# A hybrid decoder trunk: when the last down weights are split, where six bias products stand, and how the modulation products are spread

## The chip, the cores and the metric

The kernel runs on one core of a Trainium2 chip. The metric is the device time of one launch in microseconds, from the inputs in DRAM to the output in DRAM, as a median of several runs. The engines are TensorE (PE), VectorE (DVE), ScalarE (ACT), GpSimd (POOL) and SyncE (SP), which issues most of the transfers.

## What is computed

One layer on x with 512 positions and 2048 features, all in f32. A vector c gives six modulation vectors of 2048 values each; the rest is two residual blocks and a final norm.

```python
mod = silu(c) @ ada_w + ada_b          # shift1, scale1, gate1, shift2, scale2, gate2
h = rms_norm(x, g1) * (1 + scale1) + shift1
q, f, i, g, u = split(h @ w_in)        # 4 x 1024 and 1024 columns
y_a = hgrn2(q, f, i, g)                # 8 heads, chunkwise recurrence
y_b = multi_scale_pool(u)              # trailing means, windows 2, 4, 8, 16
x = x + gate1 * (concat(y_a, y_b) @ w_out)
h = rms_norm(x, g2) * (1 + scale2) + shift2
a, v = split(h @ w_up)                 # 2 x 5632 columns
x = x + gate2 * ((silu(causal_conv3(a)) * v) @ w_down)
out = rms_norm(x, g_final)
```

## The kernel before

All data lie with features on the 128 partitions and the 512 positions along the free axis. Every f32 product is made of three products of rounded halves (`mm3`, L138): each operand is split into a high part, cast on ACT, and a low part, subtracted on DVE. Weights of 128 x 1024 are split by `split_weights` (L107, lines 110 and 111 in the profile), activations and the last weights by `split` (L164, lines 166 and 167). A tile of 128 outputs is summed over k in one PSUM bank and then evicted by DVE or ACT.

The program is written as one straight order. A scheduler places each instruction on its engine by that order and by when its operands and buffers are expected to be free; on the chip each engine then runs its own queue in order. The buffers that matter: nine raw buffers of 128 x 1024 f32, 512 KB each (`rp`, L43), which hold every loaded weight, the rows of the vector products, broadcast vectors and the output blocks; three pairs of split weights (`wp`, L44); 73 tiles of 128 x 512 (`tp`, L42).

The stages, in the order of time:

- The modulations are vector products: `ada_tile` (L99) loads 1 MB of `ada_w` as two raw buffers through `gemv` (L90), and DVE multiplies each by the broadcast silu(c) and sums along the free axis (L95). `adaq` (L555) lists them. `mk_side` (L557) returns a function that the matrix loops call after every four k steps; with `adas=0.25` every fourth call makes one modulation product (`ada_next`, L568).
- The input projection, in several parts. Its last part makes the gate g in eight tiles of 16 k steps (L634 to L640), with the recurrence of the heads pumped between.
- The output projection in two passes of 16 tiles with 8 k steps each. Pass 1 (L646 to L667) takes the pooled half, adds gate1 times the sum to x and reads x again from DRAM; pass 2 (L681 to L689) takes the recurrent half, and also makes the sum of squares and the scaled, split input `h2` of the next block.
- The up projection begins with NP0 = 3 plain tile pairs (`up_mm`, L694, 96 x 3 matmuls of 512 columns over the three k parts of each pair). They work on x scaled but not shifted, so that each of their six output rows needs a bias afterwards: the product of the weights with shift2. `bias2` (L867) makes it, again through `gemv`; the first call also broadcasts shift2 over the partitions (`bcast_vec`, L521: a transpose on PE, a copy, a store to DRAM and two loads into raw buffers). Beside plain pair 1 the generator `make_a` (L822) makes the normed input, beside pair 2 `make_h` (L835) makes the seven operands of the next stage in seven steps.
- The other 41 pairs run in groups of seven half products (`up_group`, L898, in the order `SEQ` = P1, Q5, P2, P7, Q3, P6, Q4, each 24 matmuls of 256 columns). `Fast` (L727) loads, adds and splits their weights at written steps ahead; one addition per operand is made by an accumulating load from GpSimd (L766). After P2 and Q3 of the groups 1 to 5 one item of the list `todo` (L894) runs: two calls of `bias2` and then `late` (L878), the convolution and gate of a plain pair, for each of the three pairs.
- The down projection in five chunks of 10, 10, 10, 10 and 4 k blocks (`JD`, L22). In the first four, `Down.get` (L950) loads a unit of eight blocks six units ahead and splits it three ahead. The last chunk works on the two halves of the positions in turn, with 16 features of 12 matmuls of 256 columns each. In its first half every second feature loads and splits one unit of weights (L1026 to L1030); the second half uses them again. Then come the final norm and the stores.

Lines of this text and of the profile are those of the kernel before.

Of the kernel before, what the change touches and what calls it, by code (L numbers as in the profile page):

```python
# [8 lines left out]
F32 = mybir.dt.float32  # L9
# [3 lines left out]
ALU = mybir.AluOpType  # L13

P = 128
T = 512
# [19 lines left out]
def trunk_kernel(ctx: ExitStack, tc: tile.TileContext, x, c, ada, w_in, w_qft, pool_w, w_out, w_up, w_dn, cst, msk, out):  # L36
# [52 lines left out]

    def gemv(src, vec):  # L90
        a = sp.tile([P, 2], F32, tag="acc", bufs=4, name="acc")
        for i in range(2):
            r = rp.tile([P, U], F32, tag="raw", name="raw")
            nc.sync.dma_start(r, src[:, i * U:(i + 1) * U])
            V.scalar_tensor_tensor(out=r, in0=r, scalar=1.0, in1=vec[i], op0=ALU.mult, op1=ALU.mult,  # L95
                                   accum_out=a[:, i:i + 1])
        return a
# [535 lines left out]
    gs = []  # L633
    sd = mk_side(pumps=1, adas=0.25, pools=1)  # L634
    for hd in range(8):
# [9 lines left out]
    hs = [split(ys.pop(k)) for k in range(NH, 2 * NH)]  # L645
    sd = mk_side(pumps=1, adas=0.25)  # L646

# [32 lines left out]

    sd = mk_side(adas=0.5)  # L681
    ssa = tt()
# [182 lines left out]
    vec2 = []  # L865

    def bias2(i):  # L867
        if i == 0:
            vec2.append(bcast_vec(mods[3]))
        a = gemv(w_qft[KT + i], vec2[0])  # L870
        V.tensor_tensor(biases[:, KT + i:KT + i + 1], a[:, 0:1], a[:, 1:2], op=ALU.add)
        V.tensor_scalar(raws[i], raws[i], biases[:, KT + i:KT + i + 1], None, ALU.add)
        if i == 2 * NP0 - 1:
            vec2.clear()

    ad = dp.tile([NJ, P, T], F32, tag="ad", name="ad", bufs=1)

    def late(jj):  # L878
        nc.sync.dma_start(ad[jj], glu(jj, raws[2 * jj], raws[2 * jj + 1]))
        raws[2 * jj] = raws[2 * jj + 1] = None  # L880

    for jj in range(NP0):
        pr = up_mm(h2, mid if jj == 0 else None, (lambda: next(ma, None)) if jj == 1 else (lambda: next(mh, None)) if jj == 2 else None)
        for o in pr:
            z = tt()
            V.tensor_tensor(z, o, rb2[0], op=ALU.mult)
            raws.append(z)
        while jj == 0 and len(adaq) > KT:
            ada_next()
        if jj == NP0 - 2:  # L890
            fast.upto(-5)
    h2.clear()

    todo = []  # L894
    for jj in range(NP0):
        todo += [partial(bias2, 2 * jj), partial(bias2, 2 * jj + 1), partial(late, jj)]

    def up_group(n):  # L898
# [3 lines left out]
        for i in SEQ:  # L902
# [20 lines left out]
            elif i == Q4:  # L923
                V.tensor_tensor(a[:, 256:], Z, u, op=ALU.add)
            if n and i in (P2, Q3) and todo:
                todo.pop(0)()
        return n + NP0, a, v
# [64 lines left out]
    def x1_load(f):  # L992
        if f < KT:
            x1[f] = tt()
            nc.sync.dma_start(x1[f], x1d[f])

    ada_next()
    x1_load(0)
    act_more(JD[0] // 2)
    j0 = 0  # L1000
    for ci, n in enumerate(JD[:-1]):
        nxt = sum(JD[:ci + 2]) // 2
        for f in range(KT):
            o = mm_ps() if f % 2 else sm_ps()
            for k in range(n):
                wH, wL = dn.get()
                mm3(o, wH, wL, *dact[k], k == 0, k == n - 1)
            if ci == 0:
                ada_next()
                x1_load(f + 1)  # L1010
            if f >= 4 and f % 2 == 0:
                act_more(min(nxt, npair[0] + 1))
            V.scalar_tensor_tensor(out=x1[f], in0=o, scalar=mods[5][:, f:f + 1], in1=x1[f], op0=ALU.mult, op1=ALU.add)
        act_more(nxt)
        del dact[:n]
    exp_ln_table()
    ssa = tt()
    ws = []
    HT = T // 2
    n = JD[-1]  # L1020
    for hf in range(2):
# [3 lines left out]
        for f in range(KT):  # L1025
            if hf == 0 and f % 2 == 0:  # L1026
                u = NDS + f // 2
                dn.load(u + 5)
                r = dn.raw.pop(u)
                ws += [split(r[:, i * T:(i + 1) * T]) for i in range(2)]  # L1030
            wH, wL = ws[f]
# [97 lines left out]
```

## Time and profile before

| | us |
|---|---|
| median of 3 runs | 2163.57 (2163.12 to 2168.79) |
| the profiled execution | 2163.58 |
| its span | 2161.8 |
| PE busy | 2104.5 (97%) |
| PE weight loads busy | 1887.9 (87%) |
| DVE busy | 1554.1 (72%) |
| ACT busy | 921.8 (43%) |

The span runs from the first to the last instruction of the profiled execution; the execution's own time is 1.8 us more. Matmuls overlap in the records, so a busy share of PE says little about how many of them were issued; the number of matmuls in a stretch, against the number in an undisturbed stretch of the same shape, says more. The granted clock is that of TensorE, 1.00 being 2.4 GHz.

### The profile page before, as it was taken

Reading aid. Unit: us, or ns where it says so; the run is one execution under the profiler, and the core shown is the slowest. Engines: PE = TensorE matmul, PEld = TensorE weight load, DVE = VectorE, ACT = ScalarE, POOL = GpSimd, SP = SyncE. Lnnn points to the kernel's source line nnn. Section 1 sums busy time; section 2 is a strip of 40 time slices with the busy share of each in tenths; the row PEclk is TensorE's granted clock in tenths of the full one; section 3 lists DMA queues with packets and bytes.
Section 4 is the critical chain, followed back from the end, with each engine's and each line's share of the span. In section 5 each row is a group of like instructions: output and inputs, shape, how many; then the busy total and the mean of one; then the engine's idle time right before and its main releaser. Section 6 shows DMA issues by size and latency. Waiting matters only on the chain.

```text
span 2161.8 us, 32660 instructions
## 1 busy us (share of the span) xinstructions
PE 2104.5 (97%) x13010; PEld 1887.9 (87%) x13010; DVE 1554.1 (72%) x2311; ACT 921.8 (43%) x1328; POOL 95.3 (4%) x123
## 2 busy tenths in 40 slices
PE   7999999999999999899999999999999999999987
PEld 6888888888887789899999999999998888888876
DVE  8897889887778878877777777777778753333335
ACT  4314465556433364444444444444444222222234
POOL 0100000000000000000000000000000000000001
PEclk9999999999999999999999999999999999999998
DMA  9886877544578636876666666666668963333302
GB/s 369 310 306 222 268 243 260 191 157 145 186 235 275 220 86 182 239 197 161 178 173 161 177 173 163 176 175 161 172 176 307 329 226 127 117 127 115 105 5 79
DMA packets 127641, 414.66 MB, mean 192 GB/s; under 512 B 13536, under 2 KB 17920, under 8 KB 127488
## 3 DMA queue, kind: packets, MB, share of 16 engines
q1 hardware_dynamic: 115680, 369.57, 50.3%
q0 software_dynamic: 11808, 43.00, 12.1%
q8 instruction: 102, 1.67, 0.3%
q14 instruction: 51, 0.42, 0.1%
HBM read 392.58 MB, written 19.94 MB: 191 GB/s over the span
## 4 chain that ended last, share of the span: by engine, by line
PE 78%; DVE 9%; DMA 9%; issue 2%; ACT 2%; SPq 0%; DVEq 0%; ACTq 0%
PE mm L139 9%; DMA raw<-in_dram 9%; PE mm L141 8%; PE mm L140 8%; PE mm L798 7%; PE mm L797 7%; PE mm L796 7%; PE sm L798 5%; PE sm L797 5%; PE sm L796 5%; PE sm L141 4%; PE sm L139 4%; PE sm L140 4%; DVE raw L95 2%; DVE wl L111 2%
## 5 line engine op out<-in xcount | busy, mean ns | idle before, releaser
L110 ACT CAST wh<-raw 128x1024 fp32r<-128x1024 f32 x491 | 515.0, 1049 | 950.3 <-PE mm L140 291.2
L111 DVE TENSOR_TENSOR wl<-raw,wh 128x1024 fp32r<-128x1024 f32 x491 | 600.1, 1222 | 342.7 <-ACT wh L110 339.2
L139 PE MATMUL mm<-hh,wh 128*128 128x512 f32 x1120 | 437.0, 397 | 13.6 <-ACT wh L110 12.9
L141 PE MATMUL mm<-hh,wl 128*128 128x512 f32 x1120 | 438.4, 392 | 6.1 <-DVE wl L111 6.0
L140 PE MATMUL mm<-hl,wh 128*128 128x512 f32 x1120 | 436.6, 390 | 0.0
L798 PE MATMUL mm<-hh,wl 128*128 128x256 f32 x1312 | 373.2, 284 | 11.1 <-DVE wl L111 11.1
L797 PE MATMUL mm<-hl,wh 128*128 128x256 f32 x1312 | 372.7, 284 | 0.3 <-DVE hl L167 0.3
L796 PE MATMUL mm<-hh,wh 128*128 128x256 f32 x1312 | 372.6, 284 | 0.0
L95 DVE SCALAR_TENSOR_TENSOR raw<-raw,ca 128x1024 f32<-128x1024 f32 x192 | 232.5, 1222 | 70.8 <-DMA raw<-in_dram 69.8
L798 PE MATMUL sm<-hh,wl 128*128 128x256 f32 x984 | 278.7, 283 | 0.1
L796 PE MATMUL sm<-hh,wh 128*128 128x256 f32 x984 | 278.5, 283 | 0.0
L797 PE MATMUL sm<-hl,wh 128*128 128x256 f32 x984 | 278.5, 283 | 0.0
L798 PEld LDWEIGHTS mm<-hh,wl 128*128 128x128 f32 x1312 | 253.2, 193 | 12.1 <-DVE wl L111 12.1
L139 PEld LDWEIGHTS mm<-hh,wh 128*128 128x128 f32 x1120 | 210.9, 188 | 57.1 <-ACT wh L110 12.9
L141 PEld LDWEIGHTS mm<-hh,wl 128*128 128x128 f32 x1120 | 210.8, 188 | 54.1 <-DVE wl L111 9.6
L797 PEld LDWEIGHTS mm<-hl,wh 128*128 128x128 f32 x1312 | 253.3, 193 | 0.6 <-DVE hl L167 0.5
L796 PEld LDWEIGHTS mm<-hh,wh 128*128 128x128 f32 x1312 | 253.2, 193 | 0.0
L140 PEld LDWEIGHTS mm<-hl,wh 128*128 128x128 f32 x1120 | 211.1, 188 | 42.9 <-issue 0.5
L798 PEld LDWEIGHTS sm<-hh,wl 128*128 128x128 f32 x984 | 188.9, 192 | 0.5 <-DVE wl L111 0.5
L797 PEld LDWEIGHTS sm<-hl,wh 128*128 128x128 f32 x984 | 188.9, 192 | 0.0
L796 PEld LDWEIGHTS sm<-hh,wh 128*128 128x128 f32 x984 | 188.9, 192 | 0.0
L140 PE MATMUL sm<-hl,wh 128*128 128x512 f32 x384 | 149.4, 389 | 0.0
(197 smaller groups left out, 2556.1 us busy)
## 6 DMA issues: line engine op xcount, KB each, us to landing
raw<-in_dram SPq DMA_DIRECT2D x612, 512.0 KB, 4.6
raw<-in_dram POOLq DMA_DIRECT2D x82, 512.0 KB, 5.4
ad<-t SPq DMA_DIRECT2D x44, 256.0 KB, 3.0
raw<-ad SPq DMA_DIRECT2D x22, 512.0 KB, 3.7
t<-in_dram SPq DMA_DIRECT2D x32, 256.0 KB, 5.9
x1d<-t SPq DMA_DIRECT2D x16, 256.0 KB, 5.6
t<-x1d SPq DMA_DIRECT2D x16, 256.0 KB, 6.1
out_dram<-ob SPq DMA_DIRECT2D x8, 512.0 KB, 3.3
```

The lines of the kernel that those rows point to most:

```text
L95: V.scalar_tensor_tensor(out=r, in0=r, scalar=1.0, in1=vec[i], op0=ALU.mult, op1=ALU.mult, accum_out=a[:, i:i + 1])
L110: A.copy(h, r)
L111: V.tensor_tensor(l, r, h.bitcast(F32), op=ALU.subtract)
L139: E.matmul(o, wH, mH, start=start, stop=False)
L140: E.matmul(o, wH, mL, start=False, stop=False)
L141: E.matmul(o, wL, mH, start=False, stop=stop)
L796: E.matmul(o, wH[:, sl], mH, start=first and k == 0, stop=False, skip_group_check=True)
L797: E.matmul(o, wH[:, sl], mL, start=False, stop=False, skip_group_check=True)
L798: E.matmul(o, wL[:, sl], mH, start=False, stop=k == 7, skip_group_check=True)
```

## The change

Weights of the last chunk: a function `ws_next` loads and splits one unit, two features. It is called in the fourth chunk after the features 6, 8, 10, 12 and 14, and in the last chunk at every even feature, where it has work only at 0, 2 and 4 of the first half. The load limit at a call is one unit lower than before.

Bias products: `gemv` is parted into loading (`gemv_load`) and multiplying. The broadcast of shift2 is made at the end of plain pair 0. Of the six bias products, the first two are made beside pair 1 after the four steps of `make_a`, the next two beside pair 2 ahead of `make_h`, and the last two in the groups 2 and 4, their loads after P1 and their products after Q4. `make_h` has four of its seven steps beside pair 2; the other three are made in group 0 where their operand is needed. The addition of the bias to the rows moves into `late`, which stands in the groups 1, 3 and 5 after P7.

Modulation products: the rates go from 0.25 to 0.35 beside the gate tiles, from 0.25 to 0.5 in pass 1, and from 0.5 to 0.2 in pass 2. With 32 calls in each of these stages that is 11, 16 and 6 products instead of 8, 8 and 16.

```diff
--- before.py
+++ after.py
@@ -87,11 +87,15 @@
 
     mods = [cp.tile([P, KT], F32, name=f"mod{i}") for i in range(6)]
 
-    def gemv(src, vec):
+    def gemv_load(src):
+        rs = [rp.tile([P, U], F32, tag="raw", name="raw") for _ in range(2)]
+        for i, r in enumerate(rs):
+            nc.sync.dma_start(r, src[:, i * U:(i + 1) * U])
+        return rs
+
+    def gemv(src, vec, rs=None):
         a = sp.tile([P, 2], F32, tag="acc", bufs=4, name="acc")
-        for i in range(2):
-            r = rp.tile([P, U], F32, tag="raw", name="raw")
-            nc.sync.dma_start(r, src[:, i * U:(i + 1) * U])
+        for i, r in enumerate(rs or gemv_load(src)):
             V.scalar_tensor_tensor(out=r, in0=r, scalar=1.0, in1=vec[i], op0=ALU.mult, op1=ALU.mult,
                                    accum_out=a[:, i:i + 1])
         return a
@@ -631,7 +635,7 @@
     for _ in bgen:
         pass
     gs = []
-    sd = mk_side(pumps=1, adas=0.25, pools=1)
+    sd = mk_side(pumps=1, adas=0.35, pools=1)
     for hd in range(8):
         o = mm_ps()
         std_tile(hs, o, side=sd)
@@ -643,7 +647,7 @@
 
     x1 = []
     hs = [split(ys.pop(k)) for k in range(NH, 2 * NH)]
-    sd = mk_side(pumps=1, adas=0.25)
+    sd = mk_side(pumps=1, adas=0.5)
 
     def gate_silu():
         silu_batch([(t, 0.0) for t in gs])
@@ -678,7 +682,7 @@
     def scaled(k):
         h2.append(split_scaled(x1[k], a2[:, k:k + 1]))
 
-    sd = mk_side(adas=0.5)
+    sd = mk_side(adas=0.2)
     ssa = tt()
     for f in range(KT):
         o = mm_ps()
@@ -864,36 +868,52 @@
     ma, mh = make_a(), make_h()
     vec2 = []
 
+    bload = {}
+
+    def bias_load(i):
+        if i < 2 * NP0:
+            bload[i] = gemv_load(w_qft[KT + i])
+
     def bias2(i):
-        if i == 0:
-            vec2.append(bcast_vec(mods[3]))
-        a = gemv(w_qft[KT + i], vec2[0])
+        a = gemv(None, vec2[0], bload.pop(i))
         V.tensor_tensor(biases[:, KT + i:KT + i + 1], a[:, 0:1], a[:, 1:2], op=ALU.add)
-        V.tensor_scalar(raws[i], raws[i], biases[:, KT + i:KT + i + 1], None, ALU.add)
         if i == 2 * NP0 - 1:
             vec2.clear()
 
     ad = dp.tile([NJ, P, T], F32, tag="ad", name="ad", bufs=1)
 
     def late(jj):
+        for i in (2 * jj, 2 * jj + 1):
+            V.tensor_scalar(raws[i], raws[i], biases[:, KT + i:KT + i + 1], None, ALU.add)
         nc.sync.dma_start(ad[jj], glu(jj, raws[2 * jj], raws[2 * jj + 1]))
         raws[2 * jj] = raws[2 * jj + 1] = None
 
+    sides = [None, [lambda: next(ma, None)] * 4 + [partial(bias_load, 0), partial(bias2, 0), partial(bias_load, 1), partial(bias2, 1)],
+             [partial(bias_load, 2), partial(bias2, 2), partial(bias_load, 3), partial(bias2, 3)]]
+
+    def side2():
+        q = sides[jj]
+        if q:
+            q.pop(0)()
+        elif jj == NP0 - 1:
+            next(mh, None)
+
     for jj in range(NP0):
-        pr = up_mm(h2, mid if jj == 0 else None, (lambda: next(ma, None)) if jj == 1 else (lambda: next(mh, None)) if jj == 2 else None)
+        pr = up_mm(h2, mid if jj == 0 else None, side2 if jj else None)
         for o in pr:
             z = tt()
             V.tensor_tensor(z, o, rb2[0], op=ALU.mult)
             raws.append(z)
-        while jj == 0 and len(adaq) > KT:
-            ada_next()
+        if jj == 0:
+            while len(adaq) > KT:
+                ada_next()
+            vec2.append(bcast_vec(mods[3]))
         if jj == NP0 - 2:
             fast.upto(-5)
     h2.clear()
 
-    todo = []
-    for jj in range(NP0):
-        todo += [partial(bias2, 2 * jj), partial(bias2, 2 * jj + 1), partial(late, jj)]
+    todo = {(1, P7): partial(late, 0), (2, P1): partial(bias_load, 4), (2, Q4): partial(bias2, 4), (3, P7): partial(late, 1),
+            (4, P1): partial(bias_load, 5), (4, Q4): partial(bias2, 5), (5, P7): partial(late, 2)}
 
     def up_group(n):
         b = new_banks()
@@ -922,8 +942,8 @@
                 V.tensor_tensor(v[:, :256], W, u, op=ALU.subtract)
             elif i == Q4:
                 V.tensor_tensor(a[:, 256:], Z, u, op=ALU.add)
-            if n and i in (P2, Q3) and todo:
-                todo.pop(0)()
+            if (n, i) in todo:
+                todo.pop((n, i))()
         return n + NP0, a, v
 
 
@@ -993,6 +1013,15 @@
         if f < KT:
             x1[f] = tt()
             nc.sync.dma_start(x1[f], x1d[f])
+
+    ws = []
+
+    def ws_next():
+        u = NDS + len(ws) // 2
+        if u < w_dn.shape[0]:
+            dn.load(u + 4)
+            r = dn.raw.pop(u)
+            ws.extend(split(r[:, i * T:(i + 1) * T]) for i in range(2))
 
     ada_next()
     x1_load(0)
@@ -1010,12 +1039,13 @@
                 x1_load(f + 1)
             if f >= 4 and f % 2 == 0:
                 act_more(min(nxt, npair[0] + 1))
+            if ci == len(JD) - 2 and f >= 6 and f % 2 == 0:
+                ws_next()
             V.scalar_tensor_tensor(out=x1[f], in0=o, scalar=mods[5][:, f:f + 1], in1=x1[f], op0=ALU.mult, op1=ALU.add)
         act_more(nxt)
         del dact[:n]
     exp_ln_table()
     ssa = tt()
-    ws = []
     HT = T // 2
     n = JD[-1]
     for hf in range(2):
@@ -1023,11 +1053,8 @@
         xf = [x1[f][:, c0] for f in range(KT)]
         sl2 = []
         for f in range(KT):
-            if hf == 0 and f % 2 == 0:
-                u = NDS + f // 2
-                dn.load(u + 5)
-                r = dn.raw.pop(u)
-                ws += [split(r[:, i * T:(i + 1) * T]) for i in range(2)]
+            if f % 2 == 0:
+                ws_next()
             wH, wL = ws[f]
             o = (mm_ps() if f % 2 else sm_ps())[:, :HT]
             for k in range(n):
```

## Rows read from the trace of the kernel before

**Rows 1.** Page, part 1: busy us, share, instructions of each engine.

```profile
PE 2104.5 (97%) x13010; PEld 1887.9 (87%) x13010; DVE 1554.1 (72%) x2311; ACT 921.8 (43%) x1328; POOL 95.3 (4%) x123
```

**Rows 2.** Windows: stretch, length, engines' busy us (instructions), PE clock, DMA share, GB/s.

```profile
540.00:638.00 98.00, 98.00 (x489) 81.13 (x488) 73.46 (x120) 40.65 (x63) 0.00 (x0) 1.00 0.63 204
638.00:733.00 95.00, 88.91 (x386) 71.44 (x385) 77.37 (x123) 29.65 (x40) 0.00 (x0) 1.00 0.86 279
798.20:818.00 19.80, 19.01 (x154) 18.53 (x154) 19.58 (x25) 14.18 (x22) 1.74 (x2) 1.00 0.65 160
818.00:930.00 112.00, 101.33 (x810) 100.11 (x810) 91.00 (x128) 49.76 (x66) 8.63 (x10) 0.97 0.76 211
941.00:1001.00 60.00, 60.00 (x503) 60.00 (x502) 43.40 (x51) 28.51 (x36) 5.20 (x6) 1.00 0.66 170
1988.00:2076.50 88.50, 88.50 (x392) 73.31 (x391) 29.06 (x31) 18.13 (x19) 0.00 (x0) 1.00 0.28 89
2076.50:2119.40 42.90, 30.87 (x169) 28.09 (x167) 21.37 (x40) 18.46 (x41) 0.00 (x0) 0.80 0.00 0
2122.70:2147.00 24.30, 24.30 (x200) 23.99 (x198) 17.67 (x41) 14.53 (x33) 3.64 (x4) 1.00 0.26 88
```

**Rows 3.** Waits of PE, whole span: line, releaser, us in total, times, longest.

```profile
PE mm L139 <- ACT wh L110: 12.9, 1, 12.9
PE mm L798 <- DVE wl L111: 11.1, 5, 5.0
PE sm L139 <- ACT hh L166: 10.7, 7, 1.5
PE mm L141 <- DVE wl L111: 6.0, 4, 2.0
```

**Rows 4.** Timeline of PE, last chunk: start, us, instruction, [idle before, releaser].

```profile
2081.09 0.38 PE L139 MATMUL sm<-hh 128*128 128x256 f32 x1 [1.53 <-ACT hh L166]
...
2087.82 0.41 PE L139 MATMUL sm<-hh 128*128 128x256 f32 x1
2088.03 0.41 PE L140 MATMUL sm<-hl,hh 128*128 128x256 f32 x1
...
2122.84 0.28 PE L141 MATMUL mm<-hh,hl 128*128 128x256 f32 x1
```

**Rows 5.** Timeline of ACT, last chunk.

```profile
2078.67 0.42 ACT L172 ACTIVATE t<-t 128x256 f32<-128x256 f32 x1 [16.14 <-DVE t L1036]
...
2080.43 0.60 ACT L166 CAST hh<-raw 128x512 fp32r<-128x512 f32 x1
```

**Rows 6.** Timeline of DVE, fast groups.

```profile
845.40 1.23 DVE L95 SCALAR_TENSOR_TENSOR raw<-raw,sb 128x1024 f32<-128x1024 f32 x1 [3.72 <-DMA raw<-in_dram]
```

**Rows 7.** Waits of DVE, 818 to 930.

```profile
DVE raw L95 <- DMA raw<-in_dram: 12.8, 7, 3.7
```

**Rows 8.** Windows of single groups of products, columns as in rows 2.

```profile
838.00:858.00 20.00, 16.22 (x123) 16.01 (x122) 14.90 (x23) 9.44 (x13) 0.86 (x1) 0.91 0.82 220
858.00:878.00 20.00, 18.50 (x154) 18.30 (x153) 16.98 (x25) 9.65 (x13) 1.73 (x2) 1.00 0.76 203
900.00:925.00 25.00, 20.02 (x155) 19.82 (x155) 19.38 (x29) 8.77 (x11) 1.73 (x2) 0.93 0.80 237
```

**Rows 9.** Timeline of DVE, plain up tiles.

```profile
766.34 1.23 DVE L111 TENSOR_TENSOR wl<-raw,wh 128x1024 fp32r<-128x1024 f32 x1 [8.64 <-ACT wh L110]
770.49 1.23 DVE L111 TENSOR_TENSOR wl<-raw,wh 128x1024 fp32r<-128x1024 f32 x1 [2.92 <-ACT wh L110]
```

**Rows 10.** By line, DVE, 638 to 733: count, busy us, mean ns, idle before.

```profile
L95 DVE SCALAR_TENSOR_TENSOR raw<-raw,ca 128x1024 f32<-128x1024 f32 x27 | 33.1, 1224 | 18.2 <-DMA raw<-in_dram 18.0
...
L104 DVE SCALAR_TENSOR_TENSOR mod<-acc,cs 128x1 f32<-128x1 f32 x14 | 3.0, 216 | 0.2
L95 DVE DVE_READ_ACCUMULATOR raw<-raw,ca 128x1 f32 x27 | 2.2, 83 | 0.0
```

**Rows 11.** Groups by line, DVE, 541 to 638, columns as in rows 10.

```profile
L95 DVE SCALAR_TENSOR_TENSOR raw<-raw,ca 128x1024 f32<-128x1024 f32 x18 | 22.0, 1223 | 16.3 <-DMA raw<-in_dram 16.1
```

## The prediction, made before the changed kernel was run

> **What bounds the kernel now.** I read first the page's busy times: TensorE (PE) is busy 2104.5 of 2161.8 us [rows 1], so whatever the change does off PE counts only where PE waits or runs slowly. Next I cut the span into the kernel's stages and compared matmul counts, because a busy share hides both late issue and a slow clock [rows 2]. Undisturbed stages give the pace: 503 matmuls of 256 columns in 60 us (0.1193 us each) and 392 of 512 columns in 88.5 us (0.2258 us each). Against that pace three stages fall short. Pass 2 of the output projection (638 to 733) has 386 where 95 us would hold 420.7: 7.9 us lost. The fast up groups from 818 to 930 have 810 where 112 us would hold 938.8: 15.4 us lost. The first half of the last down chunk issues its 192 matmuls from 2076.5 to 2122.96, which is 46.4 us instead of 22.9 us at 0.1193 (23.3 us at the 24.3/200 of the second half): 23.3 us lost. PE's waits name what is late [rows 3]: splits of weights (L111, L166) in all three stages; the 12.9 us are the start, which the change leaves alone.
>
> The Trainium skill (Perfetto Trace Analysis, Identifying the Most-Contended Engine) says matmul busy time is a poor measure of TensorE's headroom and offers the weight loads' share instead. The trace agrees: in the last chunk PE shows 30.87 us busy of 42.9, so by busy time 12.0 us could be won there, by the count 23.3.
>
> **Last chunk.** Seven times PE waits 1.53 us for the cast of the next weights, and after such waits the matmuls start 0.21 us apart instead of 0.12, the granted clock of the stretch being 0.80, a mix of 2.4 and 1.2 GHz [rows 2 to 4]. ACT had been idle for 16.14 us before that, yet cast the pair for f = 2 only after two Squares of the chunk [rows 5]: the split is late by its place in the queue, not by its data. The change writes five of the eight pair splits into the fourth chunk (f = 6, 8, ..., 14) and the other three at f = 0, 2, 4 of the last, each ten features before its use: ten times 12 matmuls of 0.1193 are 14.3 us of lead. The waits at f = 2 to 8 must go; those at f = 10 to 14 should. The fourth chunk pays ten casts of 0.60 us [rows 5] and as many subtracts, beside DVE busy 29.06 and ACT 18.13 of 88.5 us [rows 2]: nothing for PE. The loads ask for up to ten units at once from nine raw buffers (L43), on SP's queue ahead of nothing but later units; main splits run three units, some 16 us, ahead of PE, so a load that waits for a buffer stays covered. DVE did 21.37 us of work in the slow stretch with most of the splits in it [rows 2]; with three pairs left it fits into 23 us, so PE stays the bound. If all seven waits and the slow clock go, 23.3 us come back; if only four of seven, 13.3. I take **-22.5**, near the upper end, since nothing in those rows but the split makes PE wait.
>
> **Fast groups.** Six bias products stand there now. DVE runs in order and sits on a product's load up to 3.72 us [rows 6], 12.8 us in seven waits [rows 7]; behind it are the weight subtracts PE needs. Loss is uneven [rows 8]: 838 to 858, with two products and a late GLU, is short by 44.7 matmuls (5.3 us); 858 to 878, with one product, by 13.7 (1.6 us); 900 to 925, with two products back to back, by 54.6 (6.5 us). The change leaves two, alone in groups 2 and 4, their loads issued six products earlier. I price them as the single one, 2 x 1.6 us, rounded to 3.4: **-12.0**. Bounds: -15.4 if the early loads hide everything, -2.4 if each still costs 6.5. The bias additions only move into the late GLUs, same count.
>
> **Plain up tiles and group 0.** Four products, the transpose, the copy and three DMAs of the broadcast vector come here. One product is 2.8 us of DVE: 33.1 + 2.2 + 3.0 us over 13.5 modulation products, which are of the same kind [rows 10]. DVE is idle 8.64 and 2.92 us ending at 766 and 770 [rows 9], which holds the first two. The other two (5.6 us) fall into the time when DVE makes the group operands; from 798 to 818 it is busy 19.58 of 19.80 us [rows 2], so there is no cover, and their loads may add two waits of 1.83 us (12.8/7). Three of the seven operand steps are now written inside group 0, the same instructions just before their use. Between 0 and +9.3 I take **+4**. The two broadcast buffers are held from the first plain tile to group 4 instead of over the groups alone, leaving five of nine raw buffers to the weights for longer.
>
> **Modulation products.** The gate projection gets 11 for 8, pass 1 16 for 8, pass 2 6 for 16; one leaves the first down chunk. None of PE's four longest waits lies in the gate stage [rows 3]; three products there cost nothing. Pass 2 has 10 fewer, 28 us of DVE and most of 18.0 us of waiting for their loads [rows 10], and should keep pace: **-7.9** (bounds -7.9 and 0). Pass 1 becomes what pass 2 was. DVE is busy 73.46 of 98 us there with nine products [rows 2, 11]. Sixteen make 73.46 + 7 x 2.8 = 93.1 us, plus 16 x 18.0/13.5 = 21.3 us of load waits: 16 us too long, against a lead of three half units (3 x 12 x 0.2258 = 8.1 us). If two run ahead in the gate stage, 8 too long and all covered. So 0 to +8; I take **+4**.
>
> **Sum.** -22.5 - 12.0 + 4 - 7.9 + 4 = -34.4. The profiled execution took 2163.58 us, 1.8 over its span and equal to the median of the runs, 2163.57. Forecast **2129 us**, its own range 2121 to 2137; chance 0.62.
>
> **Rivals.**
> Pass 1 takes over pass 2's stall and more: for it are the 338 GB/s it would want (8.4 MB weights, 16.8 MB modulations, 4.2 MB x, over 87 us) where pass 2 moved 279 [rows 2]; against it the lead and two products run ahead. It gives +16 instead of +4: 2141. Chance 0.15.
> The groups stay slow, because the loads themselves are late whoever orders them: groups 2 and 4 still carry a product beside accumulating loads of GpSimd, and lose 5.3 and 6.5 us as their windows do now. 11.8 instead of 3.4: 2137; with the two buffers held through groups 0 and 1 up to 2142. Chance 0.08. The Trainium skill (DMA: Bandwidth & Descriptors, Issuing engines are not separate DMA queues) would have it so: transfers of different issuers interleave on the same 16 engines.
> Only the first five splits come ahead (waits at f = 10 to 14 stay): 10 us less, 2139. Chance 0.08.
> The change doesn't do what it says: the early splits wait for buffers and are made in the last chunk again. Without the 22.5 it gives 2152. Chance 0.04.
> The other side, slower than before: pass 1, where DVE stands in order behind each product's load. A tile has 6.1 us (98/16); the work is 5.8 (93.1/16). The gains outside pass 1 are 38.4 us, so PE must lose more than that there, 46.5 with the lead, or 2.9 + 0.3 = 3.2 us of waiting per product. Pass 2 shows 1.33 on average. At 4.4, two waits of 2.2, it would be +58 - 38: 2183. Chance 0.03.
>
> **How the numbers follow.** The predicted time is the forecast's. The range is 2116 (all terms at their good ends, -46.6 us, give 2117) to 2146, which takes in the first three rivals and leaves out the last two and some spill. A difference under 0.3% (6.5 us) is about what a measurement cannot tell from none: faster means below 2157. All cases but the last two are clearly faster: 0.93; same 0.04, slower 0.03.
>
> **What would show it.** Last chunk: no PE wait for L166 between its first matmul and its end, granted clock 1.00, its first half near 23 us. Groups: at most two waits of DVE for bias loads, 818 to 930 near 935 matmuls. Group 0: a wait of PE for operand subtracts of some 3 us. Pass 2 at 4.43 matmuls per us; pass 1 with DVE above 90% and a few us lost. The prediction is wrong if PE waits in the fourth down chunk, if pass 1 loses over 8 us, or if the last chunk still shows half-speed stretches.

## The result, and the profile after

| | us |
|---|---|
| median after, 4 runs | 2132.84 (2131.44 to 2133.81) |
| median before, same session | 2165.51 (2163.12 to 2168.79) |
| ratio | 0.9848, 95% interval 0.9831 to 0.9865 |
| profiled execution after, its span | 2132.24, 2130.4 |

The forecast was 2129, the range 2116 to 2146: the total is 3.8 us above the forecast. The changed kernel's lines are shifted: L95 is now L99, L111 is L115, L139 to L141 are L143 to L145, L166 and L167 are L170 and L171, L796 to L798 are L800 to L802.

The page of the changed kernel, part 1, PE (for [rows 1]): 9.8 us less busy time, although no matmul went away.

```profile
PE 2094.7 (98%) x13010; PEld 1881.3 (88%) x13010; DVE 1549.7 (73%) x2311; ACT 921.8 (43%) x1328; POOL 95.3 (4%) x123
```

Its windows, with the columns of [rows 2]: both passes of the output projection, group 0 and its worst part, the next groups, the two halves of the last down chunk.

```profile
541.00:647.00 106.00, 106.00 (x523) 87.83 (x522) 85.28 (x149) 42.44 (x66) 0.00 (x0) 1.00 0.72 246
647.00:729.00 82.00, 79.98 (x352) 65.56 (x351) 54.64 (x78) 28.12 (x38) 0.00 (x0) 1.00 0.62 202
794.86:825.20 30.34, 25.58 (x171) 24.00 (x170) 28.41 (x41) 16.27 (x26) 1.74 (x2) 0.83 0.46 117
806.50:822.00 15.50, 10.97 (x54) 9.71 (x54) 14.58 (x21) 5.41 (x8) 0.86 (x1) 0.67 0.40 99
828.00:930.00 102.00, 101.68 (x848) 101.47 (x847) 84.31 (x110) 51.93 (x68) 8.63 (x10) 1.00 0.75 206
2067.50:2091.00 23.50, 23.50 (x196) 23.43 (x195) 15.67 (x34) 15.33 (x34) 0.00 (x0) 1.00 0.00 1
2091.00:2115.30 24.30, 24.28 (x197) 23.81 (x196) 17.37 (x40) 13.62 (x32) 3.61 (x4) 1.00 0.26 88
```

Its waits of PE over the whole span (for [rows 3]). The casts of the last weights, 10.7 us before, and the weight subtracts of the groups, 11.1 us before, are gone; the operand subtract L171 is new, 4.5 us in group 0.

```profile
PE mm L143 <- ACT wh L114: 12.9, 1, 12.9
PE sm L801 <- DVE hl L171: 4.5, 2, 3.4
PE mm L145 <- DVE wl L115: 2.0, 2, 1.5
```

PE passes from the fourth down chunk into the last without a gap, at 0.12 us a matmul from the first one on (timeline of PE, for [rows 4]):

```profile
2067.35 0.39 PE L145 MATMUL mm<-hh,wl 128*128 128x512 f32 x1
2067.57 0.28 PE L143 MATMUL sm<-hh 128*128 128x256 f32 x1
2067.69 0.28 PE L144 MATMUL sm<-hl,hh 128*128 128x256 f32 x1
```

To see where 31.4 us of span went, I divided both traces, and those of the experiments, at the same events: the first fast matmul, the 168th after it (seven half products of 24, the length of group 0), the 840th after that (five groups), and the first and last eviction of the last down chunk. At the undisturbed 0.1193 us of [rows 2], 168 matmuls are 20.0 us and 840 are 100.2.

| us | to first fast matmul | group 0 | next five groups | to last chunk | last chunk | rest |
|---|---|---|---|---|---|---|
| before | 798.3 | 21.9 | 115.6 | 1142.5 | 69.0 | 14.6 |
| after | 794.9 | 30.1 | 101.8 | 1142.5 | 46.6 | 14.6 |
| difference | -3.4 | +8.3 | -13.8 | 0 | -22.4 | 0 |

So the last chunk gave 22.4 us, the groups 13.8, and group 0 took 8.3 back. It is the one term that is far from its forecast (+4), and most experiments are about it. The same count of 168 matmuls gives the length of each group:

| us | group 1 | group 2 | group 3 | group 4 | group 5 |
|---|---|---|---|---|---|
| before | 20.2 | 25.7 | 21.9 | 21.1 | 26.8 |
| after | 20.6 | 20.2 | 20.2 | 20.2 | 20.7 |
| `load_late` | 20.6 | 20.2 | 20.6 | 20.2 | 20.8 |
| `paired` | 20.6 | 20.2 | 20.2 | 20.2 | 25.4 |
| `four_in_groups` | 20.2 | 20.2 | 20.2 | 25.9 | 21.5 |

The last three rows are experiments of the next section. A group without any loss takes 20.2 us.

**Group 0 in the trace.** PE waits 3.42 us for an operand subtract of DVE, later 1.11 us again. Behind the first wait matmuls start 0.21 us apart, not 0.12, which is the lower of the two clock levels, 1.2 GHz; the granted clock was 1.00 up to 806.5 and is 0.67, a mix of both levels, from 806.5 to 822 (windows above). Those 15.5 us hold 54 matmuls that need 6.4 at full pace: 9.1 us lost, half of it standing in the waits and half in slow matmuls. Timeline of PE:

```profile
810.62 0.58 PE L801 MATMUL sm<-hl,wh 128*128 128x256 f32 x1 [3.42 <-DVE hl L171]
811.00 0.42 PE L802 MATMUL sm<-hh,wl 128*128 128x256 f32 x1
811.21 0.41 PE L800 MATMUL sm<-hh,wh 128*128 128x256 f32 x1
...
814.76 0.58 PE L801 MATMUL sm<-hl,wh 128*128 128x256 f32 x1 [1.11 <-DVE hl L171]
```

The cause stands 25 us earlier, on DVE. The first two bias products run at 764 and 770, the first right behind the idle time that [rows 9] shows. The other two (777 to 786) fall in among the operand steps (L846, L854, L171), where DVE has no room: in the kernel before it was already busy 20.66 of the 20.71 us ahead of group 0, and in the changed one it has only the 0.72 us of a load wait idle from 774.15 to 818.65, beyond the point at which group 0 is short of operands. Two of the six bias additions (L887, 0.4 us each, at 781.3 and 817.0) fall in there too, though they are written in group 3. Windows, before and then after, and the timeline of DVE beside the plain up tiles:

```profile
777.55:798.26 20.71, 20.71 (x93) 17.13 (x92) 20.66 (x33) 11.26 (x18) 0.00 (x0) 1.00 0.26 74
```

```profile
774.15:818.65 44.50, 39.74 (x216) 34.78 (x215) 43.77 (x65) 21.39 (x34) 2.75 (x3) 0.90 0.54 154
```

```profile
762.93 1.23 DVE L115 TENSOR_TENSOR wl<-raw,wh 128x1024 fp32r<-128x1024 f32 x1 [8.80 <-ACT wh L114]
764.08 1.22 DVE L99 SCALAR_TENSOR_TENSOR raw<-raw,sb 128x1024 f32<-128x1024 f32 x1
...
777.10 1.22 DVE L99 SCALAR_TENSOR_TENSOR raw<-raw,sb 128x1024 f32<-128x1024 f32 x1
...
778.85 1.22 DVE L99 SCALAR_TENSOR_TENSOR raw<-raw,sb 128x1024 f32<-128x1024 f32 x1
...
782.86 1.22 DVE L99 SCALAR_TENSOR_TENSOR raw<-raw,sb 128x1024 f32<-128x1024 f32 x1
...
784.80 1.23 DVE L99 SCALAR_TENSOR_TENSOR raw<-raw,sb 128x1024 f32<-128x1024 f32 x1 [0.72 <-DMA raw<-in_dram]
```

### The profile page after: what moved, and what is told of

It reads as the page before. It is cut to its first block, busy times and chain, and to the rows that moved or that the text cites. A ratio compares the mean times of both kernels' runs of the same rounds, so it can differ in the third digit from the quotient of the medians.

```text
span 2130.4 us, 32653 instructions
## 1 busy us (share of the span) xinstructions
PE 2094.7 (98%) x13010; PEld 1881.3 (88%) x13010; DVE 1549.7 (73%) x2311; ACT 921.8 (43%) x1328; POOL 95.3 (4%) x123
## 4 chain that ended last, share of the span: by engine, by line
PE 86%; DMA 6%; DVE 5%; issue 2%; ACT 1%; SPq 0%; DVEq 0%; ACTq 0%; POOLq 0%
PE mm L143 10%; PE mm L145 10%; PE mm L144 10%; PE mm L800 7%; PE mm L802 7%; PE mm L801 7%; DMA raw<-in_dram 6%; PE sm L801 5%; PE sm L800 5%; PE sm L802 5%; PE sm L144 4%; PE sm L143 4%; PE sm L145 4%; PE sm L348 1%; DVE wl L115 1%
## 5 line engine op out<-in xcount | busy, mean ns | idle before, releaser
L115 DVE TENSOR_TENSOR wl<-raw,wh 128x1024 fp32r<-128x1024 f32 x491 | 599.6, 1222 | 347.7 <-ACT wh L114 345.4
L143 PE MATMUL mm<-hh,wh 128*128 128x512 f32 x1120 | 437.6, 397 | 13.7 <-ACT wh L114 12.9
L145 PE MATMUL mm<-hh,wl 128*128 128x512 f32 x1120 | 438.3, 391 | 2.1 <-DVE wl L115 2.0
L800 PE MATMUL mm<-hh,wh 128*128 128x256 f32 x1312 | 371.4, 283 | 0.3 <-ACT th L932 0.3
L802 PE MATMUL mm<-hh,wl 128*128 128x256 f32 x1312 | 371.4, 283 | 0.0
L99 DVE SCALAR_TENSOR_TENSOR raw<-raw,ca 128x1024 f32<-128x1024 f32 x192 | 231.8, 1219 | 72.2 <-DMA raw<-in_dram 72.0
L800 PE MATMUL sm<-hh,wh 128*128 128x256 f32 x984 | 280.1, 285 | 0.0
L802 PE MATMUL sm<-hh,wl 128*128 128x256 f32 x984 | 279.9, 284 | 0.0
L143 PEld LDWEIGHTS mm<-hh,wh 128*128 128x128 f32 x1120 | 211.2, 189 | 57.4 <-ACT wh L114 12.9
L145 PEld LDWEIGHTS mm<-hh,wl 128*128 128x128 f32 x1120 | 211.0, 188 | 48.6 <-DVE wl L115 3.6
L800 PEld LDWEIGHTS mm<-hh,wh 128*128 128x128 f32 x1312 | 251.8, 192 | 0.8 <-ACT th L932 0.5
L802 PEld LDWEIGHTS mm<-hh,wl 128*128 128x128 f32 x1312 | 251.9, 192 | 0.1
L800 PEld LDWEIGHTS sm<-hh,wh 128*128 128x128 f32 x984 | 190.2, 193 | 0.4 <-ACT hh L170 0.2
L802 PEld LDWEIGHTS sm<-hh,wl 128*128 128x128 f32 x984 | 190.4, 194 | 0.1
```

The source lines that it names most:

```text
L115: V.tensor_tensor(l, r, h.bitcast(F32), op=ALU.subtract)
L143: E.matmul(o, wH, mH, start=start, stop=False)
L145: E.matmul(o, wL, mH, start=False, stop=stop)
L800: E.matmul(o, wH[:, sl], mH, start=first and k == 0, stop=False, skip_group_check=True)
L802: E.matmul(o, wL[:, sl], mH, start=False, stop=k == 7, skip_group_check=True)
```

## The experiments

Theory A: group 0 is late because of the amount of DVE work that stands beside pair 2, ahead of its operands. Theory B: because three of the seven operand steps are written into group 0 and are made late. Later a third joined: the broadcast buffers, held longer, starve the weights of raw buffers. The experiments were run in three sets of four, each on one chip together with the kernel before, whose medians were 2162.53, 2162.76 and 2159.67.

### One part alone, three kernels

`ws_only`: the kernel before with the early splits and nothing else.

```diff
+            if ci == len(JD) - 2 and f >= 6 and f % 2 == 0:
+                ws_next()
...
-            if hf == 0 and f % 2 == 0:
...
+            if f % 2 == 0:
+                ws_next()
```

> The kernel before with the change to the last chunk's weights alone. If the splits' place in the queue was all that held the last chunk, its first half falls from 45 us to about 22 us and nothing else moves: about 2141 us, 22 to 23 us less than before. If the parts of the change depend on each other (raw buffers, order of the queues), it comes out more than 3 us from that.

Measured: 2140.84, ratio 0.9909 (0.9890 to 0.9929), that is -21.7 us. The last chunk takes 46.6 us as in the changed kernel, and its casts are gone from the waits of PE while those of the groups stay:

```profile
PE mm L139 <- ACT wh L110: 12.9, 1, 12.9
PE mm L798 <- DVE wl L111: 9.0, 4, 3.5
PE mm L141 <- DVE wl L111: 2.9, 3, 1.6
```

`bias_only`: the kernel before with the bias part (`gemv_load`, `sides`, the new `todo`, the additions in `late`).

```diff
-    todo = []
-    for jj in range(NP0):
-        todo += [partial(bias2, 2 * jj), partial(bias2, 2 * jj + 1), partial(late, jj)]
+    todo = {(1, P7): partial(late, 0), (2, P1): partial(bias_load, 4), (2, Q4): partial(bias2, 4), (3, P7): partial(late, 1),
+            (4, P1): partial(bias_load, 5), (4, Q4): partial(bias2, 5), (5, P7): partial(late, 2)}
```

> The kernel before with the bias products moved and the loading parted from the multiplying, nothing else. The traces of before and after put the groups after group 0 at some 14 us won and group 0 at some 8 us lost: if both belong to this part, it is 5 to 6 us faster, about 2158 us. If the loss in group 0 comes from the modulation products having been shifted, it is 12 to 14 us faster, about 2150 us.

Measured: 2158.61, ratio 0.9987 (0.9975 to 1.0000), -3.9 us, with an interval that reaches no change at all. The trace says more: group 0 takes 30.1 us and the next five groups 102.6, so the part wins 13.0 and loses 8.2, as in the changed kernel.

`rates_only`: the kernel before with the three new rates.

```diff
-    sd = mk_side(pumps=1, adas=0.25)
+    sd = mk_side(pumps=1, adas=0.5)
...
-    sd = mk_side(adas=0.5)
+    sd = mk_side(adas=0.2)
```

> The kernel before with the three new rates of modulation products alone. The forecast's terms were -7.9 us in pass 2 and +4 us in pass 1: about 2160 us. If pass 1 carries its products without a loss, as the trace of after suggests, pass 2's 7.9 us come back nearly whole: about 2157 us. If DVE in pass 1 is held by late loads as pass 2 was, no gain: 2164 us.

Measured: 2159.0, ratio 0.9982 (0.9968 to 0.9996), -3.5 us. Group 0 takes 21.8 us: the rates have no part in its loss. The three parts add up: -21.7 - 3.9 - 3.5 = -29.1, where `h_beside` below, which has all three, has -29.5 on the same chip. The changed kernel itself has -32.7 in the result above and -27.8 on another chip (`after_again`), so a sum to a few microseconds is all that this shows.

### Group 0: order or work

`h_beside`: the changed kernel with operand steps also beside the last two products, so that all seven are written beside pair 2.

```diff
-        elif jj == NP0 - 1:
+        if jj == NP0 - 1:
             next(mh, None)
```

> The changed kernel, but all seven steps of the group operands are written beside plain pair 2 again, four of the calls making a bias product too. Theory A (work): DVE has no room for two products, 5 us, beside the operands; group 0 then loses the same 8 us as in the changed kernel, 2133 us within 2. Theory B (order): group 0 loses its time because the last three steps are written inside it and come behind other work in DVE's queue; then group 0 is back near 1 us of loss and the time is about 2126 us.

Measured: 2133.0, ratio 0.9866 (0.9848 to 0.9884), group 0 30.2 us. Theory B falls: the loss only moved. PE's long wait is now for a weight cast instead of an operand:

```profile
802.52 0.58 PE L800 MATMUL sm<-hh,wh 128*128 128x256 f32 x1 [7.42 <-ACT wh L114]
```

`four_in_groups`: the products 2 and 3 go from pair 2 into the groups, four lone products in groups 1 to 4, their loads at P1.

```diff
-             [partial(bias_load, 2), partial(bias2, 2), partial(bias_load, 3), partial(bias2, 3)]]
+             []]
...
+    todo = {(1, P1): partial(bias_load, 2), (1, P7): partial(late, 0), (1, Q4): partial(bias2, 2),
+            (2, P1): partial(bias_load, 3), (2, Q4): partial(bias2, 3), (3, P1): partial(bias_load, 4), (3, P7): partial(late, 1),
+            (3, Q4): partial(bias2, 4), (4, P1): partial(bias_load, 5), (4, Q4): partial(bias2, 5), (5, P7): partial(late, 2)}
```

> The changed kernel with the products 2 and 3 taken from plain pair 2 into the groups 1 and 2, so that the groups 1 to 4 each have one product, loaded six products earlier, and pair 2 has none. Theory A (work): group 0 loses about 1 us instead of 9, and the groups lose up to 1.6 us more for each of the two: 2126 to 2129 us. Rival (raw buffers): group 0 loses its time because the two broadcast buffers are held through it; then it stays at 9 us and the time at 2133 us or above.

Measured: 2130.35, ratio 0.9853 (0.9834 to 0.9873), between the times of the two theories. Group 0 falls to 24.2 us (-5.9), which is theory A's sign, though 2.3 us over the kernel before stay. The next five groups rise to 107.8 (+6.0), but not by the price of a product: the groups 1 to 3 hold one each and take 20.2 us. The loss lies in group 4 (25.9 us), where ACT stands for a late load of weights and PE for a copy that comes behind their cast on ACT. Timelines of ACT and PE:

```profile
887.27 1.04 ACT L114 CAST wh<-raw 128x1024 fp32r<-128x1024 f32 x1 [6.61 <-DMA raw<-in_dram]
```

```profile
888.64 0.39 PE L800 MATMUL mm<-hh,wh 128*128 128x256 f32 x1 [3.95 <-ACT th L933]
```

Whether the products brought that load late was not separated.

`early`: the broadcast ahead of plain pair 0, products 0 and 1 beside pair 0, 2 and 3 beside pair 1, none beside pair 2.

```diff
-    sides = [None, [lambda: next(ma, None)] * 4 + [partial(bias_load, 0), partial(bias2, 0), partial(bias_load, 1), partial(bias2, 1)],
-             [partial(bias_load, 2), partial(bias2, 2), partial(bias_load, 3), partial(bias2, 3)]]
+    sides = [[lambda: None] * 2 + [partial(bias_load, 0), partial(bias2, 0), partial(bias_load, 1), partial(bias2, 1)],
+             [lambda: next(ma, None)] * 4 + [partial(bias_load, 2), partial(bias2, 2), partial(bias_load, 3), partial(bias2, 3)],
+             []]
...
+    while len(adaq) > KT:
+        ada_next()
+    vec2.append(bcast_vec(mods[3]))
     for jj in range(NP0):
```

> The changed kernel with the broadcast ahead of plain pair 0, the products 0 and 1 beside pair 0, 2 and 3 beside pair 1, none beside pair 2; 4 and 5 stay in the groups. DVE had 8.8 us of one gap beside pair 0 and 1. Theory A (work): group 0 back to about 1 us of loss, groups unchanged: about 2125 us. Rival (raw buffers, held even longer): 2133 us or above.

Measured: 2127.1, ratio 0.9823 (0.9804 to 0.9842); group 0 22.9 us, 1.1 over the kernel before, the next five 101.6. The broadcast buffers are held longer still, so starving by raw buffers falls as the cause of group 0's loss; A stands.

### What a product costs in the groups

`load_late`: the changed kernel with each of the two products' loads issued at the product itself, as before the change.

```diff
+    def both(i):
+        bias_load(i)
+        bias2(i)
...
+    todo = {(1, P7): partial(late, 0), (2, Q4): partial(both, 4), (3, P7): partial(late, 1),
+            (4, Q4): partial(both, 5), (5, P7): partial(late, 2)}
```

> The changed kernel with the loads of the products 4 and 5 issued at the product instead of six products earlier; each still stands alone in its group. If the early load is what freed the groups, DVE waits for the loads again and each costs some 1.6 us: +3 us. If standing alone is what counts, the same time within 1 us.

Measured: 2133.66, ratio 0.9865 (0.9849 to 0.9881), the five groups 102.3 us instead of 101.8. Issuing the loads early is worth half a microsecond. The expected 1.6 us of waiting did come for each (2.40 us and 1.08 + 1.37 us of DVE), but almost none of it reached PE.

`paired`: the same, but both products in group 4, at P2 and Q3, as pairs of them stood before the change.

```diff
-    todo = {(1, P7): partial(late, 0), (2, Q4): partial(both, 4), (3, P7): partial(late, 1),
-            (4, Q4): partial(both, 5), (5, P7): partial(late, 2)}
+    todo = {(1, P7): partial(late, 0), (4, P2): partial(both, 4), (3, P7): partial(late, 1),
+            (4, Q3): partial(both, 5), (5, P7): partial(late, 2)}
```

> The changed kernel with the products 4 and 5 both in group 4, after P2 and after Q3, each loaded where it is used, as the last two stood before. If two products close together are the cost, the group loses some 6 us again, +6 us. If the cost came from all six together, +1 to +3 us.

Measured: 2138.77, ratio 0.9889 (0.9873 to 0.9904), the five groups 106.4 us, 4.6 more than in the changed kernel, all of it in group 5 (25.4 us), where the second product lands. Timelines of DVE and PE: DVE stands 4.01 us before the second product, with a subtract of weights behind it, and PE waits 3.74 us for that.

```profile
915.13 1.23 DVE L99 SCALAR_TENSOR_TENSOR raw<-raw,sb 128x1024 f32<-128x1024 f32 x1 [4.01 <-DMA raw<-in_dram]
...
919.15 1.22 DVE L115 TENSOR_TENSOR wl<-raw,wh 128x1024 fp32r<-128x1024 f32 x1
```

```profile
920.42 0.58 PE L802 MATMUL mm<-hh,wl 128*128 128x256 f32 x1 [3.74 <-DVE wl L115]
```

In `load_late` the longest such stand was 2.40 us and PE's waits for L115 in the same groups came to 0.4 us. So two products written close together cost 4.1 us over `load_late`, which issues its loads alike. A GLU of a plain pair (L717 and L718) lies between these two as well; how much is its share was not separated.

Distance between products is not the whole of it, because of what lies beside their loads. The kernel before has three loads that come more than 2 us late (DVE at 845.4, 868.6 and 914.1), and the one at 868.6 is not the second of a close pair: the product ahead of it stands more than 20 us earlier. All three were issued 0.9 us behind an accumulating load of GpSimd (L766) and took 7.4, 6.1 and 7.2 us to land; the late one of `paired` was issued 0.9 us behind one too and took 7.3. Of the twelve product loads of the kernel before, the six with two accumulating loads in flight took 6.1 to 8.9 us, the six with none 3.2 to 4.6. The changed kernel's four are issued where none is in flight and took 3.0 to 4.5. Timelines of POOL and SP in `paired`, then the wait at 868.6 of the kernel before:

```profile
906.92 0.86 POOL L770 DMA_DIRECT2D raw<-in_dram  x1 [15.49 <-DVE raw L764]
...
907.80 1.46 SPq L93 DMA_DIRECT2D raw<-in_dram  x2
```

```profile
868.64 1.22 DVE L95 SCALAR_TENSOR_TENSOR raw<-raw,sb 128x1024 f32<-128x1024 f32 x1 [2.06 <-DMA raw<-in_dram]
```

No experiment moved a load away from the accumulating loads and left the rest alone, so the two readings, close products and loads beside an accumulating load, are not separated.

### The better arrangement, and its limit

Four kernels on one chip: the changed one unaltered (`after_again`), two other arrangements of the products, and one with other rates.

> The changed kernel once more, as the other side of a comparison on one chip. Both theories: 2130 to 2135 us; group 0 (the first 168 fast matmuls) near 30 us instead of 20.0 at the undisturbed pace, the next 840 near 102 us.

> The broadcast of shift2 ahead of plain pair 0, two products beside pair 0, two beside pair 1, none beside pair 2. If the 8.4 us that group 0 lost are work of DVE in the wrong place: group 0 near 23 us, the whole 5 to 8 us under the changed kernel on the same chip. Rival: the first look at this arrangement was a spread between runs in the passes ahead; then the two differ by less than 3 us.

Measured: `after_again` 2131.89 (2129.94 to 2134.59), `early_again` (the arrangement `early`, unaltered) 2125.56 (2124.29 to 2125.61), ratio to before 0.9836 (0.9819 to 0.9854). It is 6.3 us faster than the changed kernel and no run of either reaches the other's range. Group 0 takes 22.9 us against 30.1. Windows of `early_again`, then of the changed kernel, over the plain pairs: the work goes from the full stretch ahead of group 0 (DVE busy 30.69 of 32 us) to one in which DVE had 9 us free; then group 0 in `early_again`, at full clock.

```profile
740.00:765.00 25.00, 25.00 (x112) 20.72 (x111) 23.56 (x37) 15.63 (x34) 0.00 (x0) 1.00 0.74 261
765.00:797.00 32.00, 30.66 (x138) 25.28 (x136) 28.68 (x45) 17.04 (x27) 1.02 (x1) 1.00 0.41 118
...
795.00:818.00 23.00, 20.95 (x170) 20.35 (x169) 22.44 (x30) 15.43 (x24) 1.74 (x2) 1.00 0.51 129
```

```profile
740.00:765.00 25.00, 25.00 (x113) 20.57 (x112) 15.71 (x21) 15.96 (x35) 0.00 (x0) 1.00 0.39 147
765.00:797.00 32.00, 32.00 (x151) 26.85 (x150) 30.69 (x51) 14.82 (x22) 1.34 (x2) 1.00 0.72 231
```

`six_early`: the arrangement `early` with all six products beside the plain pairs.

```diff
+    sides = [[lambda: None] * 2 + [partial(bias_load, 0), partial(bias2, 0), partial(bias_load, 1), partial(bias2, 1), partial(bias_load, 2), partial(bias2, 2)],
+             [lambda: next(ma, None)] * 4 + [partial(bias_load, 3), partial(bias2, 3), partial(bias_load, 4), partial(bias2, 4)],
+             [partial(bias_load, 5), partial(bias2, 5)]]
...
+    todo = {(1, P7): partial(late, 0), (3, P7): partial(late, 1), (5, P7): partial(late, 2)}
```

> As the arrangement with the early broadcast, but all six products beside the plain pairs (three beside pair 0, two beside pair 1, one ahead of the second operand step beside pair 2), none in the groups. Theory that a product standing alone costs a group almost nothing: the groups give 0.5 to 1.5 us at most, group 0 stays under 25 us, and the whole is within 2 us of the arrangement with four. Rival, that DVE is full beside the plain pairs already: group 0 goes above 27 us and the whole is 3 to 6 us slower than with four.

Measured: 2130.78, ratio 0.9864 (0.9842 to 0.9885), 5.2 us slower than `early_again`. The rival was right, though group 0 stays just under its 27 us: the groups reach the undisturbed pace (840 matmuls in 100.8 us), but DVE is fuller beside the plain pairs and group 0 is back at 26.8 us, its clock at 0.94. Windows of `six_early`, plain pairs and group 0:

```profile
740.00:765.00 25.00, 25.00 (x112) 20.69 (x111) 24.75 (x40) 15.72 (x32) 0.00 (x0) 1.00 0.84 309
765.00:797.00 32.00, 32.00 (x143) 26.50 (x142) 29.04 (x46) 14.40 (x23) 1.02 (x1) 1.00 0.69 214
...
798.10:825.20 27.10, 23.38 (x172) 22.25 (x171) 25.86 (x37) 15.93 (x26) 1.73 (x2) 0.94 0.51 134
```

`gate_8`: the changed kernel with 8 modulation products beside the gate tiles and 9 in pass 2.

```diff
-    sd = mk_side(pumps=1, adas=0.35, pools=1)
+    sd = mk_side(pumps=1, adas=0.25, pools=1)
...
-    sd = mk_side(adas=0.2)
+    sd = mk_side(adas=0.3)
```

> The changed kernel with 8 modulation products beside the gate tiles instead of 11, 16 in pass 1 and 9 instead of 6 in pass 2. Theory that DVE's time over both passes is what counts, and that the three products beside the gate tiles are why pass 1 cost TensorE nothing: three products more are 3 x 2.8 us of work and 3 x 1.3 us of load waits, 12 us, against some 10 us that DVE has left over both passes (139.9 us busy and 37.7 us waiting for loads, of 188): passes 1 and 2 take 2 to 6 us longer, 2135 to 2139 us. Rival, that the loads come earlier when fewer stand in the gate stage and nothing reaches TensorE: 2131 to 2134 us.

Measured: 2131.01, ratio 0.9862 (0.9843 to 0.9882), the same as `after_again`. My theory fell: three products more in the passes cost nothing. DVE waits less for loads, 31.4 us in 24 waits against 37.7 in 18 (541 to 729), and that is where most of their 8.4 us of work went. DVE's waits, first in `gate_8`, then in the changed kernel:

```profile
DVE raw L99 <- DMA raw<-in_dram: 31.4, 24, 2.4
```

```profile
DVE raw L99 <- DMA raw<-in_dram: 37.7, 18, 4.8
```

## Why the prediction was right, and where it was off

**Last chunk, -22.5: right.** Measured -22.4, and -21.7 alone. The predicted signs are all there: no wait of PE for L170, clock 1.00, the first half in 23.7 us (196 matmuls in the window of 23.50). The reading of [rows 4, 5], that the splits were late by their place in the queue, held: the same casts, written earlier, cost the fourth chunk nothing (1142.5 us to the last chunk in both). The rivals "first five splits only" and "doesn't do what it says" fall with that.

**Fast groups, -12.0: right in mechanism, 1.8 us short.** 828 to 930 holds 848 matmuls, where 855 would be the pace. I priced a lone product by the window 858 to 878 of [rows 8] at 1.6 us. That window held a late load (2.06 us of DVE at 868.6), not the bare price of a product: the groups 2 and 4 of the changed kernel, in which its two products run, take 20.2 us like a group without any, and the 1.0 us over `six_early` that is left lies in the groups 1 and 5. The good bound stood on the early loads; by `load_late` they are worth 0.5 us, and writing the two close together, by `paired`, costs 4.1 more. The wait signature was right: no DVE wait for a bias load is left between 794.9 and 930.

```profile
DVE wl L115 <- ACT wh L114: 16.3, 17, 1.7
DVE t L944 <- PE mm L802: 1.2, 1, 1.2
DVE th L940 <- PE sm L802: 1.1, 1, 1.1
DVE raw L764 <- DMA raw<-in_dram: 0.7, 1, 0.7
```

The rival "the groups stay slow" falls. It went by the Trainium skill (DMA: Bandwidth & Descriptors, Issuing engines are not separate DMA queues); GpSimd's accumulating loads are still there, and the groups moved 206 GB/s from 828 to 930 against 211 in [rows 2], at nearly full matmul pace. The single loads are in line with that rule: beside two accumulating loads a product's load took 6.1 to 8.9 us in the kernel before, with none 3.2 to 4.6. But it cost the groups little: the loads of the changed kernel met none, and in `load_late`, where the first product's load met two and took 6.3 us, the groups are 0.5 us longer.

**Group 0, +4: the failed step.** Measured +8.3, near the upper bound 9.3. The step saw that DVE had no cover from 798 to 818 and named the right wait (operand subtracts, 4.5 us instead of 3), but took +4 out of the bounds with no row for what would be covered. It looked at DVE's idle time only up to 770 [rows 9]; the third and fourth product began at 777, in a stretch that was full already. What stands in DVE's full stretch accounts for 6.4 us: 4.9 of the two products (5.6 in the bound), 0.72 of one load wait (3.7 in the bound), and 0.8 of two bias additions, which the prediction had move into the late GLUs; the other 1.9 us stay open. The stretch at 1.2 GHz behind the wait was left out of the price as well, but that it adds to the loss is not shown: DVE is busy without a gap there and PE waits 1.11 us for it even at that pace, and in `bias_only`, where the granted clock of group 0 is 0.89 instead of 0.83, group 0 takes the same 30.1 us.

**Passes 1 and 2, -7.9 + 4: the sum right, the parts not.** No wait of PE lies in pass 1, so its +4 was not paid. Pass 2 holds 352 matmuls of 363 at 0.2258 us: 2.5 us are still lost there, so it gave back 5.4 of 7.9. The sign "DVE above 90% in pass 1" was wrong: 85.28 of 106 us is 80%, because only 13.5 products ran within it. Pass 2 shows 4.5, so of the 22 that are written in the two passes four had run ahead of 541, in the gate stage, where the prediction had counted on two at best. DVE's multiplies in pass 1, then in pass 2:

```profile
L99 DVE SCALAR_TENSOR_TENSOR raw<-raw,ca 128x1024 f32<-128x1024 f32 x27 | 32.9, 1220 | 18.0 <-DMA raw<-in_dram 17.9
```

```profile
L99 DVE SCALAR_TENSOR_TENSOR raw<-raw,ca 128x1024 f32<-128x1024 f32 x9 | 11.0, 1225 | 19.8 <-DMA raw<-in_dram 19.8
```

The rival "pass 1 takes over" and the slower one fall: the wait per product is 1.33 us (17.9/13.5), the 1.33 that pass 2 had, far from the 3.2 that it took to lose. How much the rates bring is settled only to within some microseconds: by marks before to after it is -3.4, alone -3.5 with an interval of -0.9 to -6.9, and PE's waits for L111 or L115 in the two passes are 2.9 to 6.0 us in the three kernels with the old rates and 0.7 to 2.7 in the eleven others.

**The sum.** -34.4 was forecast; the spans give -31.4. The 3.0 us are +4.3 from group 0, -1.8 from the groups, +0.5 from the time to the first fast matmul, which holds the passes, and +0.1 from the last chunk, to rounding; most of the rest of the 3.8 is the median against the profiled execution (0.6). That the total came out so near owes something to luck: the groups gave 1.8 us more than forecast when group 0 took 4.3 more, and in the passes two wrong terms nearly cancelled.

## What to carry to other kernels

A piece of work that is late by its place in a queue costs nothing once it is written a stage ahead, where the engines have room; count the matmuls of both stages to see it. Work of an in-order engine that is moved out of a busy stretch has to land in a stretch where that engine is idle, well ahead of the next consumer: with the last of the same four products done 28 us ahead of group 0 (at 769.6 in `early`) group 0 was 2.9 us over the undisturbed pace, with it done 9 us ahead (at 786.0 in the changed kernel) 10.1. When a wait of PE is priced in a stretch where PE sets the pace, the slow matmuls behind it belong to the price: in the kernel before one wait of 3.78 us stands in group 2, which is 5.5 us too long, and one of 4.98 us in group 5, which is 6.6 us too long (granted clock 0.91 and 0.93 in the windows of [rows 8]). Where another engine sets the pace, as DVE in group 0, they are not simply added.

## What the runs showed of the hardware

- After one wait of 3.42 us PE's granted clock was 0.67 over 15.5 us, where it had been 1.00. In `six_early` waits of at most 1.5 us left it at 0.94, in `early_again` waits of up to 1.7 us at 1.00.
- A load of 512 KB takes longer beside an accumulating load of GpSimd. In the kernel before the product loads took 3.2 to 4.6 us with none in flight and 6.1 to 8.9 with two; its weight loads between 940 and 1600 us had a median of 3.5 us when none was in flight as they were issued, and 5.3 when one was.
- DVE stood 4.01 us for the load of the second of two products that are written close together, at most 2.40 us for lone ones, although both were issued right at the product.
- The time to the first fast matmul differs by 6.3 us between kernels with the same rates (792.9 to 799.2). PE's waits between 30 and 541 us come to 2.6 to 4.3 us there, and some traces have short stretches at 1.2 GHz that others lack (370 to 374: granted clock 0.57 in `paired`, 1.00 in `after_again`); a change of a few microseconds in the passes can't be read from one trace.
